# Attention in pairs of units, with TensorE's order fixed

## The chip, the cores and the metric

The kernel runs on one core of a Trainium2 chip. The metric is the device time of one execution in microseconds. The engines are TensorE (PE in the profile, with its weight loads as PEld), VectorE (DVE), ScalarE (ACT), GpSimd (POOL) and SyncE (SP, which here only issues DMAs).

## The reference

One layer of a hybrid model, 1024 tokens of width 1024, float32: a modulated norm, a projection, an mLSTM mixer (512 channels) and a dilated attention mixer (8 heads of 64) side by side, an output projection with a gated residual, and an expert-choice feed-forward of 16 experts. The part that matters here:

```python
def dilated_attention_mixer(a_q, a_k, a_v, q_norm_g, k_norm_g, rel_bias):
    q = rms_norm(heads(a_q), q_norm_g)
    k = rms_norm(heads(a_k), k_norm_g)
    v = heads(a_v)
    outs, lses = zip(*[dilated_window_attention(q, k, v, rel_bias, w, d) for w, d in DILATED_PATTERNS])
    weights = jax.nn.softmax(jnp.stack(lses), axis=0)
    o = jnp.sum(weights[..., None] * jnp.stack(outs).astype(jnp.float32), axis=0)
    return o.reshape(B, S, ATTN_WIDTH).astype(a_q.dtype)
...
    mix = jnp.concatenate([y_mlstm, y_attn], axis=-1) @ w_out[l]
    x = x + gate1 * mix
```

`DILATED_PATTERNS` are windows of 128, 512 and 2048 with dilations 1, 4 and 16. Within a window a query sees keys at multiples of the dilation, with a bias by distance, softmax and values; the patterns are joined by the softmax of their log-sums.

## The kernel before

The kernel is one program for all five engines, written with a framework that places buffers, adds the semaphores and, when it builds, also chooses the order of the instructions of each engine: it goes by the order of the program as a priority and takes what its own estimate says is ready. `keep_in_program_order` keeps one instruction in the order of the program against the others so marked; the expert stage uses it already.

The stages are the modulated norm and projection, the mLSTM mixer, attention (381 to about 561 us of the trace), the output stage (`phase_out`), the routing, and the experts, which stream the expert weights from DRAM.

Attention works on 64 units: 4 head pairs (`hp`) of 16 units each. In a head pair order 0 (the first pattern, contiguous keys) comes first with 8 units, then order 1 (the two dilated patterns in one table, keys read in steps of four) with 8; of two neighbouring units one belongs to the first head of the pair (`z` = 0), one to the second. A unit covers 256 queries and has three parts:

- `attn_A`: four score matmuls (high and low half of k for two blocks of queries) into the PSUM tile `sp` (three buffers), a VectorE operation that adds the table and takes the maximum (L825), and exponentials on ScalarE (L830), giving two tiles `p`.
- `attn_B`: four transpositions of `p` (L845) into the PSUM tile `tp` (three buffers, shared with the transpositions of q and k), and a copy to `pT`, on ScalarE for even heads and on VectorE for odd ones.
- `attn_C`, for two units at once: eight matmuls with the values (L876; each shows as two in the trace) into the PSUM tile `op`, copied out by VectorE.

In step `s` of the loop of `phase_attn` the program has A of unit s, B of unit s - 2, C of the pair s - 4 and s - 3 in even steps, then one piece of each side generator, and then one step of `mix_stream`, but not in every eighth step (`MIX`). `mix_stream` is the output projection of the mLSTM half: 16 units of four steps, each step three matmuls of 512 columns (L1071 to L1073) into the one PSUM tile `mx`. After the fourth step ScalarE copies it to the one buffer `mx_ev` (L1077), a DMA on POOL's queue adds the residual input x into it (L1078), and a DMA on SP's queue stores it to `part_d` (L1079). The first two calls of each half of gate1 (`ada_rows`, four calls) stand ahead of it, and so do the splits of its operands into high and low parts. 67 loop steps less 8 leave 59 calls; 64 steps and the four of `ada_rows` make 68. What is left is run in `phase_out`, ahead of the attention half of the projection.

The side generators are the transpositions of q and k for the next head pair (`attn_pair_T`), the merge of the two orders of the head pair before (`attn_merge`: statistics to DRAM and back in another order, weights, a transposition, `w_d` to DRAM, `wb` back by broadcast, then multiplications and an addition), and the rows of gate2. At fixed steps the loop also loads and norms q and k of the next head pair and loads its tables and values; the squares of the norm and the raw tables share one buffer (`qk_sq`).

`phase_out` starts the last merge, runs what is left of `mix_stream`, and then the projection of the four attention head pairs k = 0 to 3 for the first three row blocks; k = 3 needs the last merge. Behind k = 1 it loads `xres` from `part_d`.

## Time and profile before

| | |
|---|---|
| median of three runs | 1841.47 us (1836.42 to 1842.91) |
| profiled execution | 1833.95 us, span 1832.0 us |
| mean granted TensorE clock | 0.982 |
| busy: TensorE, weight loads | 1722.9 us (94%), 1402.8 us (77%) |
| busy: VectorE, ScalarE, POOL | 1487.1 us (81%), 1197.7 us (65%), 180.5 us (10%) |

The span runs from the first to the last instruction; the time of the execution is a little longer. A busy share is a mean over stages that have different limits. Matmuls are pipelined and their ends are modelled, so two of them overlap in the trace, and what one costs is read from the distance of their starts.

### The profile page before, as it was taken

Reading aid. Unit: us, or ns where it says so; the run is one execution under the profiler, and the core shown is the slowest. Engines: PE = TensorE matmul, PEld = TensorE weight load, DVE = VectorE, ACT = ScalarE, POOL = GpSimd, SP = SyncE. Lnnn points to the kernel's source line nnn. Section 1 sums busy time; section 2 is a strip of 40 time slices with the busy share of each in tenths; the row PEclk is TensorE's granted clock in tenths of the full one; section 3 lists DMA queues with packets and bytes.
Section 4 is the critical chain, followed back from the end, with each engine's and each line's share of the span. In section 5 each row is a group of like instructions: output and inputs, shape, how many; then the busy total and the mean of one; then the engine's idle time right before and its main releaser. Section 6 shows DMA issues by size and latency. Waiting matters only on the chain. (4 is left out here: it accounts for less than half of the span.)

```text
span 1832.0 us, 24429 instructions
## 1 busy us (share of the span) xinstructions
PE 1722.9 (94%) x8696; PEld 1402.8 (77%) x8696; DVE 1487.1 (81%) x2156; ACT 1197.7 (65%) x1603; POOL 180.5 (10%) x185
## 2 busy tenths in 40 slices
PE   5999999989998939999999999999999999999997
PEld 4777888778886827888888778777787777777785
DVE  5578885687866788988988898888898888888886
ACT  5346454377763537787777777776776776777764
POOL 1001000031123020010110000100000001001000
PEclk9999999999999959999999999999999999999999
DMA  9135663325557768999999999999999999999892
GB/s 325 42 114 172 213 215 98 110 80 116 135 129 227 258 255 336 359 354 382 410 363 345 373 345 379 372 335 390 352 369 384 357 364 387 329 382 368 311 391 67
DMA packets 152553, 517.26 MB, mean 282 GB/s; under 512 B 33163, under 2 KB 50833, under 8 KB 116721
## 3 DMA queue, kind: packets, MB, share of 16 engines
q1 hardware_dynamic: 138560, 478.92, 70.7%
q0 software_dynamic: 10960, 36.32, 7.5%
q8 instruction: 68, 1.11, 0.2%
q10 hardware_dynamic: 2912, 0.48, 0.2%
q14 instruction: 53, 0.43, 0.1%
HBM read 488.16 MB, written 27.50 MB: 281 GB/s over the span
## 5 line engine op out<-in xcount | busy, mean ns | idle before, releaser
L1505 DVE TENSOR_TENSOR wl<-w,wh 128x2048 fp32r<-128x2048 f32 x278 | 627.8, 2285 | 81.6 <-ACT wh L1489 81.2
L1489 ACT ACTIVATE wh<-w 128x2048 fp32r<-128x2048 f32 x278 | 523.1, 1919 | 55.2 <-PE py L1524 26.3
L1505 DVE TENSOR_TENSOR wl<-w_half,wh 128x1024 fp32r<-128x1024 f32 x210 | 245.6, 1217 | 8.6 <-ACT wh L1489 8.5
L1489 ACT ACTIVATE wh<-w_half 128x1024 fp32r<-128x1024 f32 x210 | 211.8, 1058 | 24.1 <-PE px L1524 13.1
L1524 PE MATMUL py<-wl,xTh 128*128 128x512 f32 x512 | 139.9, 394 | 7.7 <-DVE wl L1505 7.7
L1524 PE MATMUL px<-wl,xTh 128*128 128x512 f32 x512 | 139.7, 394 | 4.5 <-DVE wl L1505 4.5
L1524 PE MATMUL px<-wh,xTh 128*128 128x512 f32 x512 | 141.1, 395 | 2.3 <-ACT xTh L124 2.1
L1524 PE MATMUL py<-wh,xTh 128*128 128x512 f32 x512 | 140.8, 394 | 2.2 <-ACT wh L1489 2.0
L1524 PE MATMUL py<-wh,xTl 128*128 128x512 f32 x512 | 138.3, 390 | 0.0
L1524 PE MATMUL px<-wh,xTl 128*128 128x512 f32 x512 | 138.1, 391 | 0.0
L1524 PE MATMUL px<-wh,hT 128*128 128x512 f32 x512 | 130.4, 396 | 0.1
L1524 PE MATMUL py<-wh,hT 128*128 128x512 f32 x512 | 129.0, 393 | 0.0
L1524 PEld LDWEIGHTS py<-wl,xTh 128*128 128x128 f32 x512 | 94.6, 188 | 33.4 <-DVE wl L1505 14.6
L1524 PEld LDWEIGHTS px<-wl,xTh 128*128 128x128 f32 x512 | 95.0, 188 | 29.5 <-DVE wl L1505 10.4
L1524 PEld LDWEIGHTS px<-wh,xTh 128*128 128x128 f32 x512 | 95.3, 189 | 23.9 <-ACT xTh L124 2.5
L1524 PEld LDWEIGHTS py<-wh,xTh 128*128 128x128 f32 x512 | 94.7, 188 | 24.0 <-ACT wh L1489 4.5
L1524 PEld LDWEIGHTS px<-wh,hT 128*128 128x128 f32 x512 | 95.6, 190 | 22.1 <-ACT wh L1489 2.1
L1524 PEld LDWEIGHTS px<-wh,xTl 128*128 128x128 f32 x512 | 96.7, 189 | 20.6
L1524 PEld LDWEIGHTS py<-wh,xTl 128*128 128x128 f32 x512 | 96.0, 188 | 20.4 <-DVE xTl L125 0.2
L1524 PEld LDWEIGHTS py<-wh,hT 128*128 128x128 f32 x512 | 95.0, 188 | 20.8 <-ACT wh L1489 0.7
L1581 POOL DMA_INDIRECT out_dram<-xin,idx x16 | 48.3, 3019 | 590.6 <-DVE xin L1580 590.6
L1445 POOL DMA_INDIRECT xin<-h_d,idx x16 | 37.8, 2362 | 477.9 <-DVE rg L1443 197.4
(456 smaller groups left out, 3138.2 us busy)
## 6 DMA issues: line engine op xcount, KB each, us to landing
w<-in_w_down_dram SPq DMA_DIRECT2D x95, 1024.0 KB, 8.4
w<-in_w_gate_dram SPq DMA_DIRECT2D x91, 1024.0 KB, 7.2
w<-in_w_up_dram SPq DMA_DIRECT2D x88, 1024.0 KB, 7.1
w_half<-in_w_gate_dram SPq DMA_DIRECT2D x70, 512.0 KB, 7.6
w_half<-in_w_up_dram SPq DMA_DIRECT2D x70, 512.0 KB, 7.5
w_half<-in_w_down_dram SPq DMA_DIRECT2D x66, 512.0 KB, 8.3
ada_w<-in_w_ada_dram SPq DMA_DIRECT2D x64, 256.0 KB, 3.5
wraw<-in_w_in_dram SPq DMA_DIRECT2D x20, 512.0 KB, 4.3
```

The lines of the kernel that those rows point to most:

```text
L1445: nc.gpsimd.indirect_dma_start(out=xin, out_offset=None, in_=self.h2_d, in_offset=bass.IndirectOffsetOnAxis(ap=idx[:, :1], axis=0))
L1489: act = self.nc.scalar.activation(h[:, j * m:(j + 1) * m], t, AF.Copy)
L1505: self.tc.keep_in_program_order(self.nc.vector.tensor_sub(l[:, c], t, h[:, c]))
L1524: nc.tensor.matmul(ps[c], x[:, t], y[:, o:o + 512], start=first and q == 0 and t == 0, stop=last and (q, t) == (2, FF // N - 1))
L1581: nc.gpsimd.indirect_dma_start(out=self.out, out_offset=bass.IndirectOffsetOnAxis(ap=u["idx"][:, :1], axis=0), in_=y, in_offset=None, comp ...
```

## The change

- The loop goes over pairs of units. An iteration has the A of both units, then two steps of `mix_stream`, then C of the pair three iterations back, then B of the pair of the iteration before, then two pieces of each side generator.
- The matmuls and transpositions of `attn_A`, `attn_B`, `attn_C`, `attn_pair_T` and `mix_stream` go through `pin`, which keeps them in the order of the program on TensorE. The other engines are ordered as before.
- No step of `mix_stream` is left out: 35 iterations make 70 calls.
- `p` has 8 buffers and not 6, `pT` 6 and not 3.

```diff
--- before.py
+++ after.py
@@ -49,7 +49,6 @@
 CUTS = 4
 HT = (1, 3, 5, 7)
 PAIR0 = 2, 4, 5
-MIX = 8
 SORTS = {9: (0, 3), 24: (3, 2), 39: (5, 2)}
 PUMP = 2
 G1 = 3
@@ -119,6 +118,10 @@
     def fill(self, pool, n):
 
         self.nc.gpsimd.memset(pool.tile([P, n // 4], F32, name="fill"), 0.0)
+
+    def pin(self, ins):
+
+        self.tc.keep_in_program_order(ins)
 
     def split(self, hi, lo, src):
         self.nc.scalar.activation(hi, src, AF.Copy)
@@ -778,7 +781,7 @@
             for j in (1, 0):
                 pf = psum()
                 for i in range(4):
-                    nc.tensor.transpose(pf[:, i * P:(i + 1) * P], qk[:, j, 4 * b + i, :], self.ident)
+                    self.pin(nc.tensor.transpose(pf[:, i * P:(i + 1) * P], qk[:, j, 4 * b + i, :], self.ident))
                 for z in range(2):
                     qT, kh, kl = T[z]
                     own, other = slice(AE * z, AE * (z + 1)), slice(AE * (1 - z), AE * (2 - z))
@@ -807,7 +810,7 @@
         kh4 = kh.rearrange("p (a b c) -> p c b a", b=4, c=4)
         kl4 = kl.rearrange("p (a b c) -> p c b a", b=4, c=4)
         sp = self.psp.tile([P, 2, 256], F32, name="sp")
-        u["p"] = pt = [aw.tile([P, 256], F32, name="p", bufs=6) for _ in range(2)]
+        u["p"] = pt = [aw.tile([P, 256], F32, name="p", bufs=8) for _ in range(2)]
         for j in range(2):
             i = 2 * g + j
             if order == 0:
@@ -815,8 +818,8 @@
                 ql, kwh, kwl = qT[:, i * P:(i + 1) * P], kh[:, w0:w0 + 256], kl[:, w0:w0 + 256]
             else:
                 ql, kwh, kwl = q8[:, i // 2, i % 2], kh4[:, i // 2], kl4[:, i // 2]
-            nc.tensor.matmul(sp[:, j, :], ql, kwh, start=True, stop=False)
-            nc.tensor.matmul(sp[:, j, :], ql, kwl, start=False, stop=True)
+            self.pin(nc.tensor.matmul(sp[:, j, :], ql, kwh, start=True, stop=False))
+            self.pin(nc.tensor.matmul(sp[:, j, :], ql, kwl, start=False, stop=True))
         for j in range(2):
             i = 2 * g + j
             c0, c1 = self.attn_cols(order, i)
@@ -834,7 +837,7 @@
         nc, aw = self.nc, self.aw
         order, g, pt = u["order"], u["g"], u["p"]
         tp = self.ptp.tile([P, 2, 2, P], F32, name="tp")
-        u["ts"] = ts = aw.tile([P, 2, 2, P], F32, name="pT", bufs=3)
+        u["ts"] = ts = aw.tile([P, 2, 2, P], F32, name="pT", bufs=6)
         for j in range(2):
             for w in range(2):
                 a0, a1 = w * P, (w + 1) * P
@@ -842,7 +845,7 @@
                     a0 = 64
                 if order == 0 and 2 * g + j == NT - 1 and w == 1:
                     a1 = P + 64
-                nc.tensor.transpose(tp[:a1 - a0, j, w, :], pt[j][:, a0:a1], self.ident)
+                self.pin(nc.tensor.transpose(tp[:a1 - a0, j, w, :], pt[j][:, a0:a1], self.ident))
         A = slice(0, P)
         if order == 0 and g == 0:
             cp = [(slice(0, 64), slice(0, 1), slice(0, 1)), (A, slice(0, 1), slice(1, 2)), (A, slice(1, 2), slice(0, 2))]
@@ -873,7 +876,7 @@
                     else:
                         kp = P
                         lv = pair["vs"][:, i // 2, w, zs]
-                    nc.tensor.matmul(op[zs, j * P:(j + 1) * P], lv, us[z]["ts"][:kp, j, w, :], start=(w == 0), stop=(w == 1))
+                    self.pin(nc.tensor.matmul(op[zs, j * P:(j + 1) * P], lv, us[z]["ts"][:kp, j, w, :], start=(w == 0), stop=(w == 1)))
         if order == 0:
             nc.vector.tensor_copy(self.ya[hp][:, g * 256:(g + 1) * 256], op)
         else:
@@ -948,38 +951,42 @@
         units = [dict(h=2 * hp + z, order=o, g=g) for hp in range(AH // 2) for o in range(2) for g in range(4) for z in range(2)]
         n = len(units)
         side = []
-        for s in range(n + 3):
-            if s < n:
-                u = units[s]
-                if s % 16 == 0:
-                    self.O2[s // 16] = self.m1.tile([P, S], F32, name="O2", tag="xTh", bufs=2)
-                hp = s // 16
-                if s % 16 == 4 and hp:
-                    self.attn_load_2(hp)
-                if s % 16 == 2 and hp < 3:
-                    self.attn_pair_norm(hp + 1)
-                if s % 16 == 8 and hp < 3:
-                    side.append(self.attn_pair_T(hp + 1, psum, aw if hp % 2 == 0 else self.ta))
-                if s % 16 == 13 and hp < 2:
-                    self.attn_load_qk(hp + 2)
-                if s % 16 == 12 and hp < 3:
-                    self.attn_load_1(hp + 1)
-                self.attn_A(u)
-            if s == 48:
-                side.append(self.ada_rows(aw, psum, 6, 8))
-            if 0 <= s - 2 < n:
-                self.attn_B(units[s - 2])
-            if s >= 4 and s % 2 == 0:
-                self.attn_C(units[s - 4:s - 2])
-            if s >= 19 and (s - 19) % 16 == 0 and s < n:
-                side.append(self.attn_merge((s - 19) // 16, psum))
-            for x in list(side):
+
+        for s2 in range(0, n + 6, 2):
+            for s in (s2, s2 + 1):
+                if s < n:
+                    u = units[s]
+                    if s % 16 == 0:
+                        self.O2[s // 16] = self.m1.tile([P, S], F32, name="O2", tag="xTh", bufs=2)
+                    hp = s // 16
+                    if s % 16 == 4 and hp:
+                        self.attn_load_2(hp)
+                    if s % 16 == 2 and hp < 3:
+                        self.attn_pair_norm(hp + 1)
+                    if s % 16 == 8 and hp < 3:
+                        side.append(self.attn_pair_T(hp + 1, psum, aw if hp % 2 == 0 else self.ta))
+                    if s % 16 == 13 and hp < 2:
+                        self.attn_load_qk(hp + 2)
+                    if s % 16 == 12 and hp < 3:
+                        self.attn_load_1(hp + 1)
+                    self.attn_A(u)
+                if s == 48:
+                    side.append(self.ada_rows(aw, psum, 6, 8))
+                if s >= 19 and (s - 19) % 16 == 0 and s < n:
+                    side.append(self.attn_merge((s - 19) // 16, psum))
+            for _ in range(2):
+                done = next(self.mix, True)
+            if 0 <= s2 - 6 < n:
+                self.attn_C(units[s2 - 6:s2 - 4])
+            if 0 <= s2 - 2 < n:
+                for u in units[s2 - 2:s2]:
+                    self.attn_B(u)
+            for x in side * 2:
                 try:
                     next(x)
                 except StopIteration:
-                    side.remove(x)
-            if s % MIX != MIX - 1:
-                done = next(self.mix, True)
+                    if x in side:
+                        side.remove(x)
         while not done:
             done = next(self.mix, True)
         for x in side:
@@ -1068,9 +1075,9 @@
                 ps = self.mix_psum()
                 for k in range(MH):
                     (h, l), (wh, wl) = hs[k], W[k]
-                    nc.tensor.matmul(ps, h[:, t], wh, start=(k == 0), stop=False)
-                    nc.tensor.matmul(ps, h[:, t], wl, start=False, stop=False)
-                    nc.tensor.matmul(ps, l[:, t], wh, start=False, stop=(k == MH - 1))
+                    self.pin(nc.tensor.matmul(ps, h[:, t], wh, start=(k == 0), stop=False))
+                    self.pin(nc.tensor.matmul(ps, h[:, t], wl, start=False, stop=False))
+                    self.pin(nc.tensor.matmul(ps, l[:, t], wh, start=False, stop=(k == MH - 1)))
                     if k < MH - 1:
                         yield False
                 ev = self.mix_ev()
```

## Rows read from the trace of the kernel before

**Rows 1.** Windows: length; busy (instructions) of PE PEld DVE ACT POOL; clock, DMA, GB/s.

```profile
400.00:554.50 154.50, 153.40 (x1102) 127.58 (x1102) 117.14 (x393) 113.78 (x335) 28.71 (x26) 1.00 0.53 121
561.00:594.30 33.30, 27.82 (x119) 21.45 (x118) 19.77 (x35) 12.42 (x22) 10.62 (x12) 0.95 0.91 274
```

**Rows 2.** Windows by head pair, columns as above (pairs 0, 1, 2, 3).

```profile
381.20:419.60 38.40, 37.24 (x254) 31.03 (x254) 33.36 (x93) 33.62 (x91) 12.74 (x10) 1.00 0.30 89
419.60:465.70 46.10, 46.10 (x339) 38.51 (x339) 36.10 (x125) 34.94 (x103) 8.05 (x7) 1.00 0.56 123
465.70:511.10 45.40, 45.40 (x305) 36.49 (x304) 37.08 (x119) 34.98 (x99) 8.44 (x7) 1.00 0.59 134
511.10:554.50 43.40, 42.30 (x333) 36.42 (x331) 29.27 (x107) 26.68 (x89) 8.61 (x9) 1.00 0.50 111
```

**Rows 3.** Timeline of TensorE, two undisturbed stretches: start us, duration, line, operation.

```profile
427.78 0.28 PE L818 MATMUL sp<-kTh,qT 128*128 128x256 f32 x1
...
432.23 0.28 PE L818 MATMUL sp<-kTh,qT 128*128 128x256 f32 x1
...
544.88 0.62 PE L845 MATMUL tp<-ident,p 128*128 128x128 f32 x4
545.43 1.09 PE L876 MATMUL op<-pT,vs 128*64 128x128 f32 x16
546.46 0.50 PE L1071 MATMUL mx<-wmh,ogh 128*128 128x512 f32 x1
...
547.27 0.38 PE L818 MATMUL sp<-kTh,qT 128*128 128x256 f32 x1
...
548.20 0.62 PE L845 MATMUL tp<-ident,p 128*128 128x128 f32 x4
...
550.28 0.29 PE L845 MATMUL tp<-ident,p 128*128 128x128 f32 x1
```

**Rows 4.** Timeline of TensorE at the end of head pair 2.

```profile
509.66 0.43 PE L876 MATMUL op<-pT,vs 128*64 128x128 f32 x2
510.02 0.44 PE L845 MATMUL tp<-ident,p 128*128 128x128 f32 x2
```

**Rows 5.** Timeline of the end of attention and the output stage, several engines.

```profile
553.36 0.42 PE L819 MATMUL sp<-kTl,qT 128*128 128x256 f32 x1
...
555.63 0.28 POOL L889 COPY st_out<-stats 128x32 f32<-128x32 f32 x1 [0.54 <-ACT p L830]
...
565.97 0.27 PE L915 MATMUL pm<-ident,me 128*32 128x128 f32 x1 [2.33 <-DVE me L912]
...
569.82 0.42 SPq L919 DMA_DIRECT2D w_d<-mw  x1
...
587.58 0.72 PE L1185 MATMUL pm<-wmh,yal 128*128 128x512 f32 x2 [1.30 <-DVE yal L125]
```

**Rows 6.** Timeline of TensorE at the start of attention.

```profile
381.20 0.38 PE L818 MATMUL sp<-kTh,qT 128*128 128x256 f32 x1 [3.55 <-ACT ev L426]
...
393.06 0.50 PE L1071 MATMUL mx<-wmh,ogh 128*128 128x512 f32 x1
...
399.89 0.51 PE L1073 MATMUL mx<-wmh,ogl 128*128 128x512 f32 x1 [1.16 <-DVE ogl L125]
```

**Rows 7.** The mx_ev buffer: timelines of ScalarE and SP, SP's waits, landing times.

```profile
475.43 0.58 ACT L1077 ACTIVATE mx_ev<-mx 128x512 f32<-128x512 f32 x1
...
481.93 0.55 SPq L1079 DMA_DIRECT2D part_d<-mx_ev  x1
...
553.36 0.57 ACT L1077 ACTIVATE mx_ev<-mx 128x512 f32<-128x512 f32 x1
...
562.55 0.60 ACT L1077 ACTIVATE mx_ev<-mx 128x512 f32<-128x512 f32 x1 [6.06 <-DMA part_d<-mx_ev]
...
SPq L1079 <- DMA mx_ev<-in_x_dram: 70.5, 13, 8.6
...
DMA to landing us min/median/max: 2.0/2.2/8.0
```

## The prediction

> **What bounds the kernel now.** I began with the busy times of the page (the table above), by which TensorE is the fullest engine over the span and VectorE the next. Such an average hides stages, so the windows by stage came next [rows 1]. The experts, the longest stage, come after all that is changed and start when their forerunners are done; I take them as shifted and not changed. The change lies in the attention stage, 381 to about 561 us, and reaches into the output stage, 561 to 594 us. From 400 to 554.5 us TensorE counts as busy for 153.4 of 154.5 us, VectorE for 117.1, ScalarE for 113.8 [rows 1]. So TensorE sets the pace and the other two have about a quarter to spare.
>
> Busy isn't the same as well used, and the third view is the windows by head pair (eight pairs of units each) [rows 2]. Head pairs 1 and 2 take 46.1 and 45.4 us, head pair 3 takes 43.4. What should they take? The TensorE timeline has undisturbed stretches [rows 3]. In one of order 0 the same point of the cycle comes back after 432.23 - 427.78 = 4.45 us, in one of order 1 after 550.28 - 544.88 = 5.40 us, each with all the work of one pair of units: eight score matmuls, six of the projection, eight transpositions, sixteen value matmuls. Four of each make 39.4 us. The transpositions of q and k for the next head pair add four groups, each no more than the 0.55 us from 544.88 to 545.43 [rows 3]: 2.2 us, so 41.6 us. Head pairs 1 and 2 are 4.5 and 3.8 us above that. A fourth view shows where this goes [rows 4]: the order in the trace isn't that of the loop but one that the build chose, in crumbs. Two value matmuls, then two transpositions: 0.36 us pass from 509.66 to 510.02 for two value matmuls, where a whole run of 16 takes 1.03 us (545.43 to 546.46 [rows 3]), 0.13 us for two. Each such cut costs some 0.2 us.
>
> **The change, part by part.**
>
> *The order pinned, in pairs.* Four runs per pair of units (8 scores, 6 projection, 16 values, 8 transpositions), against six changes of kind in the clean pairs of before. The operations themselves are the same. What two changes of kind fewer save isn't in a row alone: nothing at the least, 0.2 us each at the most (the price of a cut above), so 0 to 0.4 us per pair; I take 0.1, nearer to the clean pairs, in which each run begins without a wait: 0.8 us per head pair.
>
> *What a fixed order can't do any more* is pass over a matmul whose input is late. Values come three iterations after their scores (before: two), transpositions one after; between a pair's last score and its first transposition lie an iteration of 4.45 us or more, six projection matmuls (twice the 0.81 from 546.46 to 547.27 at most) and a run of values (1.03), about 7 us [rows 3], against a softmax that was done, and its statistics copied, 2.3 us after the last score in quiet surroundings (553.36 to 555.63 [rows 5]). That leaves over 4 us. VectorE is busy 36.1 us and ScalarE 34.9 us in head pair 1 [rows 2]; in 41 us that is 88% and 85%, and norm, q/k transposition and merge come in bursts. I give back 2 us in head pairs 1 and 2 each and 1 us in head pair 3 (bounds: 0, and the 4.5 us that the out-of-order crumbs cost now, for then nothing is won).
>
> *Larger buffers* (p 6 to 8, pT 3 to 6) cost no instruction; they only let two pairs of p and three of pT live, which the lag needs.
>
> *The start.* Projection steps stand in iteration 2 in both orders of the program, but before, TensorE did scores, transpositions and values while the operands were made: the first projection matmul ran at 393.06, and the last product of the fourth step waited 1.16 us for its operand until 399.89 [rows 6]. Pinned, the scores of pair 3 can't pass the steps of pair 2, nor values 0 those of pair 3. With fewer exponentials ahead of the splits I let the fourth step end at 398.5 instead of 399.9, then one run of values (1.03) and one of transpositions (about 0.9): pair 4 begins at about 400.4. Four pairs of order 1 and 2.2 us of q/k transpositions (23.8 us) put the end of head pair 0 at 424.2 instead of 419.6: 4.6 us lost (bounds: 2 us if the splits come as early as the scores allow, 7 us if they come no sooner and the pipeline fills behind them).
>
> TensorE would stand idle there for some 5 us. Of such gaps the trace shows both outcomes: 3.55 us idle before 381.20 [rows 6], and the clock stays at 1.00 through head pair 0 [rows 2]; 2.33 us idle before 565.97 [rows 5], and the mean of the output stage is 0.95 [rows 1], one tenth of 33.3 us at the lower level of 1.2 GHz, which costs 1.7 us. The Trainium skill (TensorE: Matmul & The Clock Gate, "HAM oscillation — how this bites in real kernels") states that gaps between bursts of matmuls put the clock back to half; it speaks against every pinned wait. By that rule the sum would be 1.7 us higher, by the first gap it would not; I leave it out of the sum and in the range.
>
> *The sum of the stage.* Head pair 0 ends at 424.2; pairs 1 and 2 take 41.6 - 0.8 + 2 = 42.8 each; pair 3, with the rows of the second gate (two groups more like 0.55) and no q/k, 40.5 - 0.8 + 1 = 40.7. That is 550.5 where the windows of before end at 554.5: 4.0 us. Both units' scores now come first in a pair, so the last ones end one pair (5.3) less eight scores (twice the 0.93 from 547.27 to 548.20 [rows 3]) ahead of that, at 547.1, and the statistics are copied 2.8 us later (the 2.3 of before, and 0.5 because two units end together), at 549.9; before, at 555.63 [rows 5]. So the last merge starts 5.7 us sooner.
>
> *The projection without the skipped step.* MIX left out every eighth call; now there are 70 calls where 68 are needed, so all 16 units of the projection end inside the loop. Before, two of them (24 matmuls, at most eight times the 0.81 us of three, 6.5 us [rows 3]) ran behind it and filled TensorE while the last merge was under way. They move from a place where they were free to a place where TensorE is the bound; the clean pairs above hold all six matmuls, so this is paid in the sum already. What the missing filler leaves behind is waiting, not work: the output stage waits for the merge. From the copy of the statistics at 555.63 to the split of the merged head at 587.58 [rows 5] pass 32 us; its matmuls for heads 0 to 2 are all but done before that (1.30 us idle ahead of 587.58).
>
> *The DMAs of those units.* Each has an add into one single mx_ev buffer, on POOL's queue, and a store, on SP's. SP waited 70.5 us for those adds, in 13 rounds [rows 7], and the last merge's w_d, of which the transposition ran at 565.97, stood behind one until 569.82 [rows 5]. With no unit left there I win 2.5 us of that. In exchange the loads of xres, which before came behind, can stand ahead of w_d and wb on SP and in the DMA engines: 0 to 4 us, I take 1.
>
> *The sum.* 5.7 + 2.5 - 1 = 7.2 us sooner for the last merge, and all behind it shifts. The profiled execution took 1833.95 us (span 1832.0), so 1826.8; the median of the runs is 7.5 us above the profiled one, so I predict 1834.3 us, 0.4% less than 1841.47. What a measurement of this kernel can tell from no change is 0.5%, 9.2 us: the likeliest case is the upper part of no change.
>
> **The rivals.**
>
> *Nothing stalls.* If bursts are covered by the lag and the start costs 2 us, 2.6 + 5 us come on top, and 0.1 us per pair more for the changes of kind, 3 us: about 18 us won at the most, some 14 as a rule, 1827 us. For it: in [rows 3] no run waits. Against it: VectorE at 88%.
>
> *VectorE and ScalarE set the pace.* The order is then only another way to wait: head pairs 1 and 2 keep their 46 us, the start costs 4.6, and the earlier scores and w_d give some back: 1841 us. For it: 36.1 and 34.9 us of work in bursts; norm and the table of order 1 share one buffer. Against it: 10 us to spare per head pair.
>
> *The single mx_ev buffer becomes the bound, and the kernel slower.* A round was 475.43 (copy) to 481.93 (store) [rows 7] and about 2.2 us to land: 8.7 us. 16 rounds have to fit into 400 to 550 us now, 9.4 us each; before there were 14. If the round grows past 9.4 us, ScalarE stands in the copy with all exponentials queued behind it (it did so once, 6.06 us, in a round of 9.2 us [rows 7]), then the projection's only PSUM buffer stays full and the pinned matmul holds up everything. Each 1 us of round is then 16 us. At 10.6 us: 19 us more than the forecast, 1853 us; it makes the kernel slower by over 0.5% from about 10.4 us. For it: SP, in order, also carries the table and value loads. Against it: 8.7 us is below 9.4.
>
> **How the numbers follow.** The forecast (1834.3) gets 0.42, a third of it beyond the 9.2 us, the rest not; nothing stalls 0.20; the others set the pace 0.20; the mx_ev round 0.18, nearly all of it slower. Faster by over 0.5%: 0.14 + 0.20 = 0.34; slower 0.17; no change 0.49. The range takes the best bounds (18 us won: 1823) and the mx_ev case just past its threshold (1851). The likeliest case's own is 1828 to 1840.
>
> **What would show it.** Right: head pairs 1 and 2 in 42 to 44 us, four long runs per pair; a gap of 3 to 7 us on TensorE around 387 to 393 us; the last exponentials at about 550; no projection behind the loop; TensorE idle for some us before the fourth head of the output stage. Wrong: ScalarE idle before mx_ev for the store (third rival); waits of TensorE for p or pT of over 2 us in each head pair (second); a stage of experts that doesn't just shift, which would undo all of this.

## The result: 0.9% slower, where 0.4% faster was forecast

| | before | after |
|---|---|---|
| median | 1840.11 us (1836.42 to 1842.91, 4 runs) | 1855.61 us (1854.44 to 1858.98, 4 runs) |
| ratio, 95% interval | | 1.0088, 1.0065 to 1.0112 |
| profiled execution | 1833.95 us | 1858.98 us |
| mean granted TensorE clock | 0.982 | 0.971 |

The profiled execution of before lies below its timed runs and that of after is the highest of its four, so the two traces differ by 25 us where the medians differ by 15.5. Sizes are therefore taken from ratios, and places from the traces.

In after, functions of attention stand 3 lines lower than in before (the scores L821 and L822, the value matmuls L879, the merge L892 to L935), the projection 7 lower (L1078 to L1080, its evacuation L1084). The windows of after come first, by head pair and then the output stage up to the addition of the merged head, with the columns of [rows 1]; they answer to [rows 2]. The last six are the stretches at the lower of the clock's two levels, 1.2 GHz (0.50 in the column of the clock).

```profile
382.20:430.80 48.60, 42.25 (x269) 35.73 (x269) 36.35 (x101) 38.83 (x103) 13.44 (x12) 0.89 0.30 81
430.80:473.70 42.90, 42.00 (x324) 35.53 (x322) 34.10 (x118) 30.77 (x91) 8.32 (x7) 1.00 0.57 131
473.70:521.50 47.80, 43.16 (x325) 36.01 (x322) 38.55 (x118) 35.34 (x102) 11.76 (x9) 0.96 0.66 149
521.50:568.80 47.30, 44.42 (x319) 37.85 (x318) 26.17 (x103) 26.02 (x90) 5.87 (x7) 0.93 0.39 92
568.80:613.90 45.10, 28.73 (x155) 22.24 (x153) 20.47 (x35) 10.00 (x17) 16.17 (x37) 0.83 0.82 251
...
383.50:390.40 6.90, 5.68 (x26) 5.64 (x27) 5.37 (x19) 5.72 (x19) 0.04 (x1) 0.51 0.00 0
397.20:400.60 3.40, 2.94 (x12) 2.48 (x12) 3.40 (x4) 2.96 (x4) 1.27 (x1) 0.50 0.61 211
503.00:506.40 3.40, 3.39 (x14) 3.30 (x15) 2.26 (x7) 3.03 (x6) 1.44 (x2) 0.50 0.42 104
537.10:544.00 6.90, 6.27 (x35) 5.75 (x36) 5.87 (x29) 4.83 (x19) 0.00 (x0) 0.51 0.36 114
581.50:591.80 10.30, 8.45 (x24) 6.52 (x24) 5.80 (x13) 3.90 (x5) 5.17 (x27) 0.50 0.88 247
608.80:619.10 10.30, 4.04 (x9) 2.76 (x10) 4.27 (x5) 1.78 (x3) 2.34 (x1) 0.50 0.74 305
```

Head pair 1 is as forecast: 42.9 us, clock 1.00, TensorE busy for all but 0.9 us. Head pair 0 takes 48.5 us (48.6 with the window's bounds rounded) instead of 38.4, 2 takes 47.8 instead of 45.4, and 3 (here up to the last exponential) 47.3 instead of 44.3. In before the clock was 1.00 in all four [rows 2]; here it falls to half in three. The timeline of TensorE shows the waits near these stretches (in brackets the idle time and what ended it), and two clean pairs of units:

```profile
382.22 0.38 PE L821 MATMUL sp<-kTh,qT 128*128 128x256 f32 x1 [3.85 <-ACT ev L429]
...
384.72 2.07 PE L1040 MATMUL tp<-ident,col_b 128*128 128x128 f32 x8 [1.29 <-DVE col_b L1036]
...
395.21 0.50 PE L1078 MATMUL mx<-wmh,ogh 128*128 128x512 f32 x1 [3.04 <-ACT wmh L127]
...
403.59 0.50 PE L1080 MATMUL mx<-wmh,ogl 128*128 128x512 f32 x1 [0.90 <-DVE ogl L128]
...
478.07 0.36 PE L821 MATMUL sp<-kTh,qT 128*128 128x256 f32 x1
...
482.42 0.36 PE L821 MATMUL sp<-kTh,qT 128*128 128x256 f32 x1
...
486.64 0.50 PE L1079 MATMUL mx<-wml,ogh 128*128 128x512 f32 x1 [1.72 <-DVE wml L128]
...
501.95 0.66 PE L784 MATMUL tp<-ident,qk 128*128 128x128 f32 x4 [2.40 <-ACT pT L860]
...
510.36 0.58 PE L821 MATMUL sp<-kTh,qT 128*128 128x256 f32 x1
...
515.99 0.57 PE L821 MATMUL sp<-kTh,qT 128*128 128x256 f32 x1
...
537.73 1.98 PE L879 MATMUL op<-pT,vs 128*64 128x128 f32 x16 [2.81 <-DVE ml L911]
...
598.67 0.27 PE L918 MATMUL pm<-ident,me 128*32 128x128 f32 x1
...
615.03 0.80 PE L1190 MATMUL pm<-wmh,mix 128*128 128x512 f32 x1 [9.94 <-ACT mix L127]
```

Near isn't always the cause. The first stretch begins at 383.5, when the wait of 1.29 us before 384.72 has only begun (384.72 - 1.29 = 383.43), and in e1_merge below, with the same order of TensorE, it begins at 381.9, 0.6 us ahead of the like wait. So that wait doesn't bring it; what lies ahead of it is the idle time of 3.85 us before the first score, which in before was 3.55 us and had no such stretch behind it [rows 6].

A clean pair of order 0 takes 4.35 us (478.07 to 482.42; 4.45 in [rows 3]), one of order 1 5.63 (510.36 to 515.99; 5.40 in [rows 3]), the one after it, up to the first score of head pair 3 at 521.47, 5.48. The last two rows, and these of the other engines, answer to [rows 5]:

```profile
536.68 0.17 DVE L905 TENSOR_TENSOR mM<-stats,st_in 128x16 f32<-128x16 f32 x1 [7.26 <-DMA st_in<-stat_d]
...
568.97 1.31 POOL L892 COPY st_out<-stats 128x32 f32<-128x32 f32 x1 [4.25 <-issue]
...
576.80 0.37 SPq L896 DMA_DIRECT2D st_in<-stat_d  x1
...
583.76 0.18 DVE L915 TENSOR_TENSOR me<-me,ml 128x16 f32<-128x16 f32 x1
...
599.28 0.32 SPq L922 DMA_DIRECT2D w_d<-mw  x1
...
613.92 1.06 ACT L127 ACTIVATE mix<-ya 128x1024 fp32r<-128x1024 f32 x1 [15.77 <-DVE ya L935]
```

In before the split of the merged head on ScalarE, the last of these rows, stood here:

```profile
586.42 1.06 ACT L124 ACTIVATE mix<-ya 128x1024 fp32r<-128x1024 f32 x1 [2.34 <-DVE ya L932]
```

The statistics of the last head pair are copied at 568.97 instead of 555.63: 13.3 us later. The last merge's weights are ready for their transposition at 583.94, but the transposition runs at 598.67. From the copy to it pass 29.7 us, where before it was 10.3 [rows 5]. Behind it w_d leaves after 0.6 us instead of 3.9, and the way from the transposition to the split of the merged head on ScalarE is 15.25 us instead of 20.45. So the merge costs 29.70 - 10.34 - 5.20 = 14.2 us, and with the 13.3 of the stage the split comes 27.5 us later (613.92 against 586.42); TensorE stands idle for 9.94 us for it, before 615.03. Of that the end gets 25.3 (span 1857.3 against 1832.0): what follows shifts, as forecast.

### The profile page after: what moved, and what is told of

It reads as the page before. It is cut to its first block, busy times and chain, and to the rows that moved or that the text cites. A ratio compares the mean times of both kernels' runs of the same rounds, so it can differ in the third digit from the quotient of the medians.

```text
span 1857.3 us, 24424 instructions
## 1 busy us (share of the span) xinstructions
PE 1725.3 (93%) x8696; PEld 1406.4 (76%) x8696; DVE 1488.7 (80%) x2156; ACT 1198.1 (65%) x1603; POOL 181.4 (10%) x185
## 5 line engine op out<-in xcount | busy, mean ns | idle before, releaser
L1588 POOL DMA_INDIRECT out_dram<-xin,idx x16 | 48.3, 3020 | 590.8 <-DVE xin L1587 590.8
```

What stands on the lines that cost most here:

```text
L1588: nc.gpsimd.indirect_dma_start(out=self.out, out_offset=bass.IndirectOffsetOnAxis(ap=u["idx"][:, :1], axis=0), in_=y, in_offset=None, comp ...
```

## The experiments

Two theories came out of this. **M**: the last merge is late, because its steps were driven by the two projection units that no longer run behind the loop. **P**: pinned matmuls wait for operands that come late, and the clock falls with the waits. The rival **E** is the third one of the prediction, the single mx_ev buffer. All kernels but after were timed in five rounds beside the kernel before, whose median on those chips was 1836.6 to 1837.3 us; 0.1% is 1.8 us. Before's 1840.11 us lies some 3 us above that, and the expectations of the first four runs, which are in us, go by it; beside their own before their bounds are to be read some 3 us lower. Ratios can be compared as they are. The lengths of head pairs (HP) are from the first score matmul of one to that of the next, of the last to the end of its exponentials, each in the one profiled execution.

| kernel | median us | ratio, 95% interval | HP 0, 1, 2, 3 (us) |
|---|---|---|---|
| before | 1840.11 | 1 | 38.4, 46.1, 45.4, 44.3 |
| after | 1855.61 | 1.0088 (1.0065 to 1.0112) | 48.5, 42.9, 47.8, 47.3 |
| e1_merge | 1840.58 | 1.0028 (1.0015 to 1.0042) | 48.3, 43.0, 46.8, 42.1 |
| e2_tail | 1841.85 | 1.0029 (1.0015 to 1.0043) | 48.4, 43.1, 47.3, 40.8 |
| e3_start | 1861.48 | 1.0133 (1.0116 to 1.0151) | 43.4, 43.1, 52.1, 42.9 |
| e4_yield | 1858.31 | 1.0121 (1.0105 to 1.0137) | 48.5, 43.3, 54.1, 40.0 |
| f1_nopin | 1839.75 | 1.0010 (1.0000 to 1.0020) | 45.1, 43.1, 47.1, 41.7 |
| f2_ev | 1841.56 | 1.0021 (1.0010 to 1.0032) | 48.2, 42.8, 46.7, 41.1 |
| f3_oldpin | 1862.61 | 1.0139 (1.0125 to 1.0154) | 51.6, 43.4, 47.8, 47.2 |
| f4_nomix | 1849.19 | 1.0063 (1.0050 to 1.0076) | 42.6, 45.6, 48.6, 45.9 |
| g2_start | 1845.72 | 1.0049 (1.0034 to 1.0065) | 43.6, 43.7, 53.4, 40.1 |
| h2_norm | 1843.56 | 1.0035 (1.0022 to 1.0047) | 48.4, 42.9, 52.9, 42.5 |
| h5_both | 1842.36 | 1.0035 (1.0022 to 1.0048) | 43.0, 43.1, 48.6, 41.2 |
| g4_nopin_tail | 1836.58 | 0.9994 (0.9980 to 1.0009) | 43.5, 43.5, 46.9, 45.9 |
| i1_w1 | 1838.98 | 1.0016 (1.0006 to 1.0026) | 47.8, 43.0, 45.2, 46.0 |
| i2_stin | 1842.43 | 1.0029 (1.0017 to 1.0042) | 48.2, 42.8, 46.7, 41.1 |
| i3_w1_start | 1837.92 | 1.0005 (0.9995 to 1.0014) | 42.4, 43.0, 45.9, 41.9 |
| i4_best | 1832.63 | 0.9984 (0.9972 to 0.9995) | 42.8, 44.6, 39.9, 46.7 |

**e1_merge**: the last merge alone.

```diff
-            for _ in self.mix:
+            for _ in range(8):
                 next(merge, 1)
```

> The changed kernel with the last merge's eight steps taken at once where the empty projection loop stands. Theory M (half of the loss is the last merge: its steps were driven by the two projection units that no longer run behind the loop, so its transposition waits behind the matmuls of three heads): the transposition comes 5 to 12 us after the statistics instead of 30, the split of the last merged head 8 to 14 us sooner, the time 1842 to 1848 us. Theory P (the pinned order alone loses it, in waits inside the attention loop): the time stays at 1853 to 1857. Rival E (the single evacuation buffer of the projection): stays too.

Measured: 1.0028, 0.60% below after, which is 11 us, and within M's bounds beside its own before. The timelines of e1_merge on POOL, TensorE and ScalarE:

```profile
561.48 0.73 POOL L892 COPY st_out<-stats 128x32 f32<-128x32 f32 x1 [4.25 <-issue]
...
575.39 0.37 PE L918 MATMUL pm<-ident,me 128*32 128x128 f32 x1 [5.48 <-DVE me L915]
...
595.12 1.06 ACT L127 ACTIVATE mix<-ya 128x1024 fp32r<-128x1024 f32 x1 [5.77 <-DVE ya L935]
```

13.9 us instead of 29.7 from the copy to the transposition, a little more than expected, and TensorE now waits for the weights and not the other way round. From the copy to the split of the merged head it is 33.6 us instead of 44.9 (568.97 to 613.92), 11.3 us less, as much as the time gained. M holds and is the larger part. TensorE's order up to the end of attention is that of after, so that this trace is also a second execution of the same loop: head pair 3 takes 42.1 us here and 47.3 there, and VectorE's wait for the statistics of the third merge is 4.7 us here and 7.3 there.

**e2_tail**: the other way to give the merge its driver back.

```diff
-            for _ in range(2):
+            for _ in range(2 if s2 < 60 else 0):
                 done = next(self.mix, True)
```

> The changed kernel with the projection's steps ended after 60, so that two of its 16 units run behind the loop, as before the change, and drive the last merge again. Theory M: the merge is back in its old place behind the statistics and the loop's last three pairs are some 4 us shorter: 1838 to 1845 us. Theory P: only the loop's end gains, 2 to 4 us: 1851 to 1854. Rival E: the same 1838 to 1845 only if ScalarE's waits for the buffer go as well.

Measured: 1.0029, within M's bounds, with 9.7 us from the copy to the transposition (560.91 to 570.57). Two units more or fewer in the loop make no difference beside that, with the pins in place.

**e3_start** and **e4_yield**, on after: the start later, the arithmetic of the first three merges later.

```diff
-            for _ in range(2):
+            for _ in range(2 if s2 >= 4 else 0):    # e3_start
...
-        for _ in range(4):
+        for _ in range(8 if hp < AH // 2 - 1 else 4):    # e4_yield
             yield 0
```

> The changed kernel with the projection's steps beginning two iterations later, so that the pinned order meets no operand that isn't made. Theory P: the 10 us lost in the first head pair mostly go (its 48.5 us become 39 to 43), the last four steps fall behind the last scores: 1846 to 1851 us. Theory M: the start is hidden by nothing and still counts, but the last merge is unchanged, so the gap from the last statistics to its transposition stays near 30 us; if M were all of it, the time stays at 1853 to 1857.

> The changed kernel with the merges of the first three head pairs begun as now but their arithmetic four steps (two pairs of units, some 10 us) later, so that VectorE does not reach it before its statistics are back from memory. Theory P: VectorE's wait of 7.3 us in the fourth head pair and TensorE's half clock behind it go, head pair 3 falls from about 48 to 41 to 44 us: 1849 to 1852 us. Theory M: no change beyond 3 us, 1852 to 1857.

Both expectations missed. Each edit does what it should in its own place (head pair 0 from 48.5 to 43.4; head pair 3 from 47.3 to 40.0, where e1_merge's 42.1 shows that 5 of the 7 us can be chance) and loses it in head pair 2, which rises from 47.8 to 52.1 and 54.1. Head pair 2 isn't all of it in e3_start: the way from the copy of the last statistics to the split also grows, from 44.9 to 48.8 us, and its profiled execution came 5 us late out of the stage before attention, which its edit doesn't explain. The windows and TensorE's timeline of e4_yield:

```profile
473.40:527.50 54.10, 45.47 (x324) 37.85 (x322) 41.62 (x124) 35.40 (x101) 10.96 (x10) 0.91 0.55 133
```

```profile
492.74 0.79 PE L1079 MATMUL mx<-wml,ogh 128*128 128x512 f32 x1 [6.40 <-DVE wml L128]
```

In head pair 2 the second half of the projection's weights is scaled and split, while VectorE norms q and k and merges head pair 1. A pinned projection matmul stands for that split, here 6.4 us (in after 1.72).

**f1_nopin**: e1_merge with nothing pinned (after with `pin` empty and the loop of e1_merge).

```diff
     def pin(self, ins):
-        self.tc.keep_in_program_order(ins)
+        pass
```

> The run e1_merge (pairs, larger buffers, no skipped step, last merge driven early) with no order pinned: the build places TensorE's instructions again. Theory P (what is left of the loss, 0.28%, is waits of pinned matmuls for operands that come late: the start and the second half's weights): the first head pair falls from 48.3 to 39 to 43 us, the third from 46.8 to 42 to 45, and the time comes 5 to 10 us below that of e1_merge, at 0.993 to 0.998 of the kernel before. Rival V (VectorE's bursts set the pace, whatever the order): within 3 us of e1_merge, 1.001 to 1.004.

Measured: 1.0010, 0.18% or 3 us below e1_merge, with intervals that overlap. That is what rival V expected of the time. P misses both head pairs: the first goes a third of the way (48.3 to 45.1 us, expected 39 to 43), the third stays at 47.1, so there it isn't the pins. The first is the more telling, for with nothing pinned 6.7 of the 10 us lost against before remain. The timeline and the window of f1_nopin at the start show that the clock falls here too:

```profile
383.28 0.39 PE L821 MATMUL sp<-kTh,qT 128*128 128x256 f32 x1 [3.62 <-ACT ev L429]
```

```profile
384.40:387.80 3.40, 3.40 (x18) 3.40 (x18) 2.70 (x17) 3.04 (x9) 0.00 (x0) 0.50 0.01 2
```

It falls 1.1 us after the first score, in an unbroken run of scores, so neither a pin nor a wait inside attention brings it; ahead of it lies the idle time that ends the stage before.

**f2_ev**: e1_merge with two mx_ev buffers.

```diff
-        self.mix_ev = lambda: mx.tile([P, 512], F32, name="mx_ev")
+        self.mix_ev = lambda: mx.tile([P, 512], F32, name="mx_ev", bufs=2)
```

> The run e1_merge with two buffers instead of one for the evacuated projection. Rival E (ScalarE standing in that copy holds up exponentials and the pinned order): 3 to 8 us below e1_merge, 0.998 to 1.001 of the kernel before. Theory P: ScalarE's wait of 5.9 us at the end goes, which is hidden in part, 0 to 3 us below e1_merge: 1.001 to 1.003.

Measured: 1.0021, as P expected, with an interval that overlaps that of e1_merge. The head pairs move by at most 1 us. E isn't the cause.

**f3_oldpin**: the kernel before with the pins (in the functions the change pins) and the larger buffers, in its own loop.

```diff
+            self.pin(nc.tensor.matmul(sp[:, j, :], ql, kwh, start=True, stop=False))
...
-        u["p"] = pt = [aw.tile([P, 256], F32, name="p", bufs=6) for _ in range(2)]
+        u["p"] = pt = [aw.tile([P, 256], F32, name="p", bufs=8) for _ in range(2)]
```

> The kernel before with its own loop, one unit at a time and every eighth projection step skipped, but with TensorE's instructions pinned to the order of the program and the larger buffers. Theory P: the pins are what costs: the same start loss of some 10 us and waits at the second half's weights, 8 to 25 us slower than before, 1.004 to 1.014. If instead the pair order and its longer lag cost, this stays within 0.997 to 1.003.

Measured: 1.0139, 25 us, P's upper bound, but not for P's reason alone. TensorE's timeline of f3_oldpin has pinned value matmuls that stand for 5.12 us in the start, and head pair 0 takes 51.6 us:

```profile
405.63 1.97 PE L880 MATMUL op<-pT,vn 128*64 128x128 f32 x14 [5.12 <-DVE pT L859]
```

From the first score to the copy of the last statistics it takes 190.2 us, before 174.4: some 16 us in the loop. The other 10 lie behind it, where the split of the merged head comes 40.9 us after the copy, before 30.8. There the copy of the last merge's weights stands on VectorE behind an operation that waits for the router's weights:

```profile
594.55 0.29 DVE L1118 TENSOR_TENSOR wra<-sort_mem,a_col 128x128 f32<-128x128 f32 x1 [8.35 <-DMA sort_mem<-in_w_router_dram]
594.76 0.27 DVE L921 COPY mw<-pm 32x128 f32<-32x128 f32 x1
```

That is no wait of a pinned matmul, so what P speaks of is nearer to 16 than to 25 us. In the pair order the pins cost less (0.18% by e1_merge against f1_nopin, 0.35% by e2_tail against g4_nopin_tail below); which of its parts does that, the runs or the longer lag, wasn't separated.

**f4_nomix**: the kernel before without the skipped step.

```diff
-            if s % MIX != MIX - 1:
-                done = next(self.mix, True)
+            done = next(self.mix, True)
```

> The kernel before with the skipped projection step taken out, nothing else: all 16 units inside the loop, none behind it to drive the last merge. Theory M: the last merge's transposition comes 25 to 32 us behind the statistics instead of 10.6, and the time rises by 8 to 14 us: 1.004 to 1.008. If the order of the merge only mattered with pins, it stays within 0.998 to 1.002.

Measured: 1.0063, 12 us. The timelines of f4_nomix on POOL and TensorE:

```profile
567.19 0.30 POOL L889 COPY st_out<-stats 128x32 f32<-128x32 f32 x1 [5.81 <-issue]
...
591.34 0.27 PE L915 MATMUL pm<-ident,me 128*32 128x128 f32 x1
```

24.2 us from the copy to the transposition, just below what M expected. The unskipped step does the same kind of harm without pins and pairs. Not all of the 12 us is that: from the copy to the split it is 38.9 us, 8 more than before, and the loop is 8 us longer too (182.8 us from the first score to the copy), as it now holds the work of two more units.

**g2_start**, **h2_norm** and **h5_both**: e1_merge with the later start of e3_start, with the norm of the last head pair moved, and with both.

```diff
+                    late = 4 if hp == 2 else 0
-                    if s % 16 == 2 and hp < 3:
+                    if s % 16 == 2 + late and hp < 3:
                         self.attn_pair_norm(hp + 1)
-                    if s % 16 == 8 and hp < 3:
+                    if s % 16 == 8 + late // 2 and hp < 3:
```

> The run e1_merge with the projection's steps beginning two iterations later (the last two steps then run directly behind the loop). Theory P (the start costs some 5 us more than forecast, because pinned matmuls stand for operands that are split later, and the clock falls): the first head pair falls from 48.3 to about 43.4 us, as it did in e3_start, and if nothing else moves the time is 3 to 5 us below e1_merge, 0.999 to 1.001 of the kernel before. Rival W (the second half's weights move by two iterations too and fall into VectorE's fullest stretch): the third head pair rises from 46.8 to 50 to 53 us and the time is that of e1_merge or above, 1.002 to 1.006.

> The run e1_merge with the normalization of the last head pair's q and k two pairs of units later and its transposition one pair later, so that in the third head pair it does not meet the split of the second half's weights and the merge on VectorE. Theory P with VectorE's burst as the late work: the wait of 1.6 us for the split weight and the half clock behind it go, the third head pair falls from 46.8 to 43 to 45 us, 2 to 3 us below e1_merge: 1.001 to 1.002. If the burst only moves (to the transposition of q and k), the third head pair stays at 46 to 48 us and the time within 1.002 to 1.004.

> The run e1_merge with both edits, the later start of the projection and the later normalization in the third head pair. Theory P: first head pair 43.4, third 43 to 45 us, 6 to 8 us below e1_merge and so below the kernel before, 0.996 to 0.999. Rival W (each shift of VectorE's work meets another): third head pair at 46 us or more, 1.000 to 1.004.

Measured: 1.0049, 1.0035, 1.0035. In g2_start rival W holds for the head pairs: the windows show that the 4.7 us of the start come back as 6.6 in head pair 2.

```profile
382.00:425.60 43.60, 39.55 (x257) 33.18 (x257) 37.31 (x101) 37.57 (x102) 13.50 (x11) 0.88 0.28 78
...
469.30:522.60 53.30, 43.98 (x323) 36.15 (x322) 38.62 (x125) 35.52 (x102) 8.39 (x7) 0.97 0.57 132
```

Of the 4.7 us, 3.2 are only less work: the start now holds four steps fewer, at 0.81 us each [rows 3]. And the loop as a whole is as long as that of e1_merge (180.9 us from the first score to the copy of the last statistics, 180.4 there); what this profile loses lies behind it, with 38.3 us from the copy to the split instead of 33.6, of which 3 us are the broadcasts of the weights (wb), 7.1 us behind w_d instead of 4.0.

h2_norm's time is in the second range that was expected, but its third head pair is in neither: the burst only moved, and to a worse place, 52.9 us. In h5_both rival W holds again, with 48.6 us there. It is the best of the pinned loops so far (175.8 us from first score to last exponential, e1_merge 180.2), and yet no faster. SP's timeline of h5_both shows where that goes: the broadcasts of the last merge's weights leave 8.6 us behind w_d, because the store of the last projection unit, now later, stands ahead of them in the queue and waits for its add.

```profile
576.44 0.38 SPq L922 DMA_DIRECT2D w_d<-mw  x1
...
584.13 0.33 SPq L1087 DMA_DIRECT2D part_d<-mx_ev  x1
...
585.02 2.37 SPq L927 DMA_DIRECT2D wb<-w_d  x4
```

**g4_nopin_tail**: `pin` empty as in f1_nopin, two units behind the loop as in e2_tail.

> The changed kernel with no order pinned and the projection's last two units left behind the loop, so that they drive the last merge: of the change only the pairs, the larger buffers and the unskipped steps before that remain. Theory P: the start as in f1_nopin (45 us for the first head pair), the loop's last pairs 3 us shorter, the merge as in e2_tail: 0.998 to 1.001. If the pair order itself costs, no better than e2_tail: 1.002 to 1.004.

Measured: 0.9994, no difference to before, as P expected. Pairs and buffers alone win nothing that shows; against e2_tail the pins cost 0.35%, 6 us, and here the two intervals don't overlap.

**i1_w1**, **i2_stin**, **i3_w1_start**: one suspected cost each left out of e1_merge and g2_start.

```diff
-            W = []
-            for k in range(MH):
+            if c == 0:
+                W = []
+            for k in range(MH if c == 0 else 0):    # i1_w1, i3_w1_start
...
-                    raws.append(self.w_half(k, 1))    # i1_w1, i3_w1_start
...
-        n2, l2 = y[:, :, 0, :], y[:, :, 1, :]
+        n2, l2 = (y[:, :, 0, :], y[:, :, 1, :]) if hp == AH // 2 - 1 else (self.st[:, 1, 0, :, hs], self.st[:, 1, 1, :, hs])    # i2_stin
```

> The run e1_merge without loading, scaling and splitting the second half's projection weights: the second half's units use the first half's weights, so that half of the output is another function, with the same matmuls on TensorE. Theory S (what is left in the third head pair is the burst of VectorE in which this split meets the normalization and the merge): the third head pair falls from 46.8 to 42.5 to 44 us, the time by 3 to 4 us, to 1.000 to 1.001 of the kernel before. Rival Q (the transposition of q and k, waiting for score buffers shared with the transposed exponentials, sets it): 46 to 47 us still.

> The run e1_merge in which the first three merges take the statistics of the second order from the place they are written to and not from memory behind the transfer, so that those three merges weigh with unpermuted statistics; the transfers still run. Theory S: the fourth head pair's wait of VectorE for the transfer goes, its 42.1 us become 40 to 41, the time falls by 0 to 2 us, to 1.002 to 1.003. If the transfer is what the changed kernel's 5 us of spread in that head pair hang on, the spread of the time falls too.

> The run g2_start (later start of the projection) without the second half's weights, as in i1_w1. Theory S: the first head pair keeps its 43.5 us and the third no longer pays for it: 43 to 45 us instead of 53.4, the time 0.997 to 0.999 of the kernel before. Rival Q: the third head pair stays above 48 us, the time at 1.002 to 1.005.

Measured: 1.0016, 1.0029, 1.0005; the first and the last are above what S expected, and below Q. The windows of i3_w1_start:

```profile
381.80:424.20 42.40, 39.56 (x255) 33.38 (x256) 35.78 (x102) 37.38 (x102) 8.60 (x9) 0.88 0.28 78
...
467.20:513.10 45.90, 42.56 (x325) 35.70 (x322) 34.99 (x119) 33.20 (x98) 8.36 (x7) 1.00 0.59 131
```

Without the second weights the later start keeps its gain, and head pair 2 falls from 53.4 to 45.9 us: the two belong together, as theory S says. In e1_merge the same takes only 1.6 us off head pair 2 (46.8 to 45.2, expected 42.5 to 44). Some 2 to 3 us above head pair 1 remain there; the norm and the transposition of q and k are left, but no run shows their share. In i3_w1_start too the whole gains less than the stage (173.2 us), for the reason seen in h5_both: wb leaves 8.9 us behind w_d, and the split comes 39.8 us after the copy, in e1_merge 33.6. The statistics' transfer is worth at most 1 us in head pair 3 and nothing that shows in the time (1.0029 against 1.0028).

**i4_best**: g4_nopin_tail with the steps of the projection two iterations later.

```diff
-            for _ in range(2):
+            for _ in range(2 if 4 <= s2 < 64 else 0):
```

> The run g4_nopin_tail (no pins, two units behind the loop) with the projection's steps beginning two iterations later and ending two later. If the start and the place of the second half's weights are the same trade without pins: within 0.2% of g4_nopin_tail, 0.998 to 1.002. If the build passes over the late weights here, the start's 2 to 4 us are won: 0.996 to 0.999.

Measured: 0.9984, 0.16% or 3 us faster than before, within the 0.5% that was called no change, but with its whole interval below 1. It lies in both of the ranges that were expected, so it doesn't decide between them.

## Why the prediction was wrong

It named the other sign, and the time lies outside its range. Point by point:

**The projection without the skipped step: the step that failed most.** "What the missing filler leaves behind is waiting, not work", it says, and counts the two units for their matmuls alone. But `for _ in self.mix` also takes one step of the last merge for each step of the projection, eight in all. With no step left, the merge moves on only with the matmuls of the output stage, and its transposition, which stands behind those of heads 0 and 1, comes 14.7 us after its input is ready (583.94 to 598.67). The price is 11 us by e1_merge, where 2.5 us had been won on w_d; f4_nomix has the same delay without pins and pairs. That smaller term was right as such (w_d leaves 0.6 us behind the transposition, before 3.9). The 1 us for the xres loads isn't shown by any run: they were to hold up w_d, which leaves at once; st_in does leave later, 7.8 us behind the copy of the statistics (568.97 to 576.80), before 5.4 (555.63 to 561.00), but there the copy itself takes 1.31 us instead of 0.28, and a store of the projection that waits for its add stands ahead on SP's queue until 575.93.

**The start: mis-sized.** 4.6 us lost were forecast (bounds 2 to 7), 10.1 came (48.5 against 38.4). The fourth step's last product was put at 398.5; it runs at 403.59. The idle time isn't what was mis-sized: some 5 us were forecast, and the waits up to 403.59 add up to 5.9. The half clock on top of them was: the first two of the six stretches hold 8.6 us of TensorE's busy time, for which the sum had nothing. And the mechanism, operands made too late for a pinned place, is the smaller part of it, for f1_nopin without any pin wins only 3.2 us back.

**The clock left out of the sum.** The prediction noted 1.7 us and took the first of two outcomes in [rows 6] and [rows 5]. It should have gone by the second. In the windows above TensorE is busy for 5.68 + 2.94 + 3.39 + 6.27 = 18.3 us at half clock in attention, so up to some 9 us of this profile's stage are the clock's and not the wait's own (estimated as half of that busy time; less where TensorE would have waited anyway); in before there were none. The Trainium skill (TensorE: Matmul & The Clock Gate, "HAM oscillation — how this bites in real kernels") has the matmuls of a kernel start cold again after each wait for a DMA between two bursts; this trace agrees in head pairs 2 and 3 and in the output stage, where waits of 2.40, 2.81, 4.99 (before 582.41) and 9.94 us have a half-clock stretch beside them, and in the start with 3.85 and 3.04 us; the 3.55 us of [rows 6] and the 1.72 us before 486.64 have none. Nor is the pinned order needed for it, as f1_nopin shows. The trace of before was a favourable one in this: its granted clock is 0.982, the median of its 96 timed runs beside the experiments 0.980, and after's four runs have 0.971 to 0.974.

**Stalls in the head pairs.** 42.8 us were forecast for head pairs 1 and 2: the first came at 42.9, the second at 47.8 (46.8 in e1_merge). That the first fits so well is in part luck: its idle time is 0.9 us and not 2, but four of each clean pair make 39.9 us (4.35 and 5.63) and not 38.6. And the pins aren't what wins there, for f1_nopin has 43.1 us without them. The 2 us given back for bursts did not hold the split of the second half's weights, which the prediction's list of bursts leaves out and which falls on the norm and the merge. That is the rival "VectorE and ScalarE set the pace" in one head pair of four; f1_nopin, at 47.1, shows that it isn't the pins, and i1_w1, at 45.2, that the split is 1.6 us of it. Head pair 3 lost 5 to 7 us (42.1 in e1_merge, 40.0 in e4_yield) around VectorE standing in the merge's first operation for a transfer, in a profile that was unlucky there; the median of after can't have all of that.

**Changes of kind.** 0.1 us per pair was taken as won, against six changes in the clean pairs of before (their rows have seven runs of one kind). Order 0 gives that (4.35 against 4.45 us); order 1 loses 0.1 to 0.2 (5.48 and 5.63 against 5.40), without a wait, for a reason that no run here shows. The four long runs came, but the clean pairs of f1_nopin have them too, so they come with the program's new order and not with the pins.

**The rivals.** The mx_ev round was the only rival with a time near the result, for the wrong reason: 16 rounds fit (ScalarE waited for the buffer's store for 2.6 us in the loop and 5.9 behind it), and a second buffer moves the time by 0.07% with overlapping intervals. The last statistics came at 569, not at 550, so nothing reached the output stage sooner. That the experts only shift was right to some us: from the addition of the merged head to the end 1243.4 us, before 1245.6; in the profiles of the experiments this stretch is 1239 to 1247 us long.

The sum by ratios: of 0.88%, 0.60 go with the merge (after to e1_merge), 0.18 with the pins (to f1_nopin) and 0.16 with the two units in the loop (to g4_nopin_tail), where 0.9994 is left. Only the first of these steps is clear of its intervals; taken in the other order the last two come out differently, with nothing for the units (e1_merge to e2_tail) and 0.35 for the pins (e2_tail to g4_nopin_tail). What stays open is why head pair 2 keeps 2 to 3 us with the weights gone, why the pins cost more in some loops than in others, and what makes up the rest of the start's loss without them.

## What to carry to other kernels

A loop over leftover work may also be the clock by which other work is advanced: before emptying it, list what each of its iterations calls, and drive that on its own. A pinned order turns each late operand into idle time of the fullest engine, so look for the places where operands are made (starts, second halves of weights), not for the mean load of the engine that makes them. And a late producer that is moved meets the next one: the later start won 4.7 us in its place and lost 6.6 in another. What is won inside a stage also has to reach its end: h5_both's loop is 4.4 us shorter than e1_merge's and its time is no better, because one store on a queue held up the broadcasts behind the loop.

## What the runs showed of the hardware

The length of one wait doesn't tell whether the clock falls beside it. In after 1.72 us of idle time before 486.64 left the clock at 1.00; in e1_merge as much, before 499.98, lies ahead of 3.4 us at the lower level, as its timeline and window show:

```profile
499.98 1.09 PE L784 MATMUL tp<-ident,qk 128*128 128x128 f32 x8 [1.72 <-ACT pT L860]
```

```profile
501.40:504.80 3.40, 3.40 (x12) 3.01 (x12) 2.81 (x7) 3.18 (x6) 1.35 (x2) 0.50 0.43 89
```

It is the same with longer ones: 3.55 us ahead of attention left the clock at 1.00 in before, 3.62 us lay ahead of its fall in f1_nopin. So a forecast can't read the clock off one trace of before.

And the way of 16 KB of statistics through DRAM isn't steady: with the same order of TensorE, VectorE stood 7.3 us for it in one execution and 4.7 us in another, and head pair 3 took 47.3 and 42.1 us. From the copy on POOL to VectorE's first operation on the statistics it was 12.7 us (524.01 to 536.68) and 10.3 us; 2.8 to 3.3 of these pass before the write leaves, behind a store of the projection on SP's queue.
